# Seven half units of a normed activation turned by way of DRAM and VectorE in a fused two-layer decoder kernel

## The chip, the cores and the metric

The kernel runs on one core of a Trainium2 chip. TensorE (PE in the profile) multiplies matrices into PSUM; VectorE (DVE) and ScalarE (ACT) work on SBUF and PSUM; SyncE (SP) issues nearly all DMAs between DRAM and SBUF. Each engine takes its instructions in a fixed order and they wait for each other through semaphores. The metric is the device time of one execution in microseconds, the median of several runs.

## The reference

Two layers on 512 tokens of width 2048 in fp32: a layer of differential attention, then one projection of the stream into shared keys, values and forget gates, then a layer of forgetting attention.

```python
def shared_kv(x, c_act, w_mod_kv, b_mod_kv, w_kv, b_f):
    mod = c_act @ w_mod_kv + b_mod_kv
    shift, scale = jnp.split(mod, 2, axis=-1)
    hk = x * (1.0 + scale[:, None]) + shift[:, None]
    kvf = hk @ w_kv
    k, v, zf = jnp.split(kvf, [B_WIDTH, 2 * B_WIDTH], axis=-1)
    ...
    log_f = jax.nn.log_sigmoid(zf.astype(jnp.float32) + b_f.astype(jnp.float32))
    F = jnp.cumsum(log_f, axis=1)

for l in range(DEPTH):                                   # DEPTH = 2, N_A = 1
    h = x * (1.0 + scale[:, None]) + shift[:, None]
    if l < N_A:
        y = diff_attention(h, ...)
    else:
        if kv is None:
            kv = shared_kv(x, c_act, kv_w_mod, kv_b_mod, kv_w, kv_b_f)
        y = forgetting_attention(h, ..., *kv)
    x = layer_norm(DN_ALPHA * x + gate[:, None] * y, ln_g[l], ln_b[l])
```

The change lies at the seam: the layer norm that ends layer 0, and the first value columns of `hk @ w_kv`.

## The kernel before

**Products.** Every fp32 matrix product is made of three fp32r products: high part by high part, high by low, low by high (`products`, L227 to L231). A weight tile of 128x1024 comes from DRAM into `wst`, ScalarE casts its high part `whi` (L117), and VectorE makes the low part `wlo` = `wst` - `whi` (L118). `whi` and `wlo` have three buffers each, used in rotation.

**The normed activation.** The out projection of layer 0 ends with four token blocks of 128. For each, `norm_a(b)` (L1123) finds mean and 1/std, ScalarE norms the first 1024 columns of `n` (L1128) and VectorE the others (L1129), and SP stores the block to `n_dram` (L1130), from where layer 1's residual reads it much later.

**Turning.** The next product needs `n` with the 2048 features on the partitions. It is cut into 16 half units (half, s): half 0 or 1 is token blocks 0 and 1 or 2 and 3, and s is one of eight pairs of feature blocks. `build_half(s, half)` (L1132) turns a half unit's four 128x128 blocks on TensorE into one PSUM bank (L1140). For each of the two feature blocks ScalarE applies the modulation twice, once to fp32 (`htmp2`, L1148) and once to the high part `hh` (L1149), and VectorE makes the low part `hl` (L1150). At the end VectorE copies the turned blocks back into `n` (L1153), since layer 1 builds its own modulated activation from them later.

**Consuming.** The first group of value columns, `vj[0]`, takes the half units in the order of `lag` (L1156): (0,0), (0,1), (0,2), (0,3), (1,0), (1,1), (1,2), (0,4), (1,3), (0,5), (1,4), (0,6), (1,5), (0,7), (1,6), (1,7). I call the twelve matmuls of one half unit a step: two token blocks, two feature blocks, three products each. Before a step the loop (L1256) calls `build_next`, which builds a half unit that comes later in the order. Half 0 takes a weight tile, half 1 takes the same one a step or more later, and at the end of a half 1 step more weights are cast (`ws.advance`). Behind this group come the other value groups and, among their matmuls, the forget logits (L1221, L1222: 64 matmuls of the bank `zfp`).

**What sets the order.** Outside the kernel's first stage, which has an order written out by hand, the code's order is not yet the engines': a scheduler of the framework places each instruction in its engine's queue. So an edit at one place can also move instructions that it doesn't name.

Of the kernel before, what the change touches and what calls it, by code (L numbers as in the profile page):

```python
# [10 lines left out]
F32 = mybir.dt.float32  # L11
F32R = mybir.dt.float32r
I32 = mybir.dt.int32
AF = mybir.ActivationFunctionType
ALU = mybir.AluOpType

P = 128
D = 2048
# [147 lines left out]
def tile_yoco(  # L166
# [23 lines left out]
    nc = tc.nc  # L190
    V, S, PE, G = nc.vector, nc.scalar, nc.tensor, nc.gpsimd
# [13 lines left out]
    n_dram = dram.tile([T, D], F32, name="n_dram")  # L205
# [8 lines left out]
    def sc_bank(name="sc"):  # L214
        return ps.tile([P, 512], F32, name=name, tag="sc", bufs=2)
# [11 lines left out]
    def products(dst, lhs, rhs, start, stop):  # L227

        PE.matmul(dst, lhs[0], rhs[0], start=start, stop=False)  # L229
        PE.matmul(dst, lhs[0], rhs[1], start=False, stop=False)  # L230
        PE.matmul(dst, lhs[1], rhs[0], start=False, stop=stop)  # L231
# [120 lines left out]
    Hh = [None] * KT  # L352
    Hl = [None] * KT

    def new_h(kt):
        Hh[kt] = hpool.tile([P, T], F32R, name="hh", tag="H")
        Hl[kt] = hpool.tile([P, T], F32R, name="hl", tag="H")
# [149 lines left out]
    with tc.tile_pool(name="start", bufs=2, reuse_waits="tile") as sp, tc.manual_schedule(engines=engines):  # L507
# [6 lines left out]
        xts, loaded, accs, pms, turned, temps, banks, hi_of = {}, {}, {}, {}, {}, {}, {}, {}  # L514
# [528 lines left out]
    def moments(pool, stats, b):  # L1043
        mv = pool.tile([P, 2], F32, name="mv", tag="mv", bufs=4)
        V.bn_aggr(mv, stats[:, b, :, :])
        ve = pool.tile([P, 1], F32, name="lve", tag="lve", bufs=4)
        rstd = pool.tile([P, 1], F32, name="lrstd", tag="lrstd", bufs=4)
        V.tensor_scalar(ve, mv[:, 1:2], EPS, None, op0=ALU.add)
        rsqrt(rstd, ve, 1, pool)
        return mv, rstd  # L1050
# [41 lines left out]
    zp = []  # L1092

    ab = {}
# [28 lines left out]
    def norm_a(b):  # L1123
        pool, n, stats = zp
        mv, rstd = moments(pool, stats, b)
        mr = pool.tile([P, 1], F32, name="mr", tag="mr", bufs=4)
        V.scalar_tensor_tensor(mr, mv[:, 0:1], -1.0, rstd, op0=ALU.mult, op1=ALU.mult)
        S.activation(n[:, b, 0:1024], n[:, b, 0:1024], AF.Identity, scale=rstd, bias=mr)  # L1128
        V.tensor_scalar(n[:, b, 1024:], n[:, b, 1024:], mv[:, 0:1], rstd, op0=ALU.subtract, op1=ALU.mult)  # L1129
        nc.sync.dma_start(n_dram[b * P : (b + 1) * P, :], n[:, b, :])  # L1130

    def build_half(s, half):  # L1132

        pool, n, _ = zp
        px = sc_bank()
        hs = slice(256 * half, 256 * half + 256)
        for q in range(2):
            for b in range(2):
                src = n[:, 2 * half + b, (2 * s + q) * P : (2 * s + q + 1) * P]
                PE.transpose(px[:, q * 256 + b * P : q * 256 + (b + 1) * P], src, ident)  # L1140
        for q in range(2):
            kt = 2 * s + q
            if half == 0:
                new_h(kt)
            tmp = pool.tile([P, 256], F32, name="htmp2", tag="htmp2", bufs=2)
            pq = px[:, q * 256 : (q + 1) * 256]
            sc, sh = ab["kv"][0][:, kt : kt + 1], ab["kv"][1][:, kt : kt + 1]
            S.activation(tmp, pq, AF.Identity, scale=sc, bias=sh)  # L1148
            S.activation(Hh[kt][:, hs], pq, AF.Identity, scale=sc, bias=sh)  # L1149
            V.tensor_tensor(Hl[kt][:, hs], tmp, Hh[kt][:, hs].bitcast(F32), op=ALU.subtract)  # L1150

        place = n[:, 2 * half : 2 * half + 2, 2 * s * P : (2 * s + 2) * P].rearrange("p b (q t) -> p q b t", t=P)
        V.tensor_copy(place, px.rearrange("p (q b t) -> p q b t", q=2, b=2))  # L1153


    lag = [(0, 0), (0, 1), (0, 2), (0, 3), (1, 0), (1, 1), (1, 2)]  # L1156
# [5 lines left out]
    def build_next(n=1):  # L1162
        for _ in range(n):
            unit = next(built, None)
            if unit:
                build_half(unit[1], unit[0])

    pieces.extend(attention_a(A_HEADS - 1, 1))
    pieces.append(lambda: split_og((14, 15)))
    pieces.append(lambda: ab.update(kv=fold(0, ktile("mrow"))))  # L1170
    out_projection(oA, 0, zp, open_n, residual_a, norm_a, lambda b, k: build_next() if b == 3 and k < 2 else None)
    npool, n, nstats = zp

# [17 lines left out]
    def evac_v(g):  # L1191
        def fn(b, acc):
            vt = ktile("vt")
            S.copy(vt, acc)
            nc.scalar.dma_start(v_dram[b * P : (b + 1) * P, 512 * g : 512 * (g + 1)], vt)
        return fn
# [59 lines left out]
    for i, (half, s) in enumerate(lag):  # L1256
        if i != 2:
            build_next()
        if (half, s) == (0, 3):
            ws.step(lambda: kpool.tile([P, 512], F32R, name="held", tag="K"))  # L1260
            ws.load(ws.done + ws.STAGES - 1)
        if half == 0:
            held[s] = ws.get(vj[0], s, 0)
        hi, lo = held[s]
        for b in (2 * half, 2 * half + 1):
            bs = slice(b * P, (b + 1) * P)
            for kq in range(2):
                kt = 2 * s + kq
                products(acc[b], (Hh[kt][:, bs], Hl[kt][:, bs]), (hi[kq], lo[kq]), kt == 0, kt == KT - 1)
            if s == KT // 2 - 1:  # L1270
                evac_v(0)(b, acc[b])
        if half == 1:
            ws.advance(ws.where[id(vj[0]), s] + 4)
# [310 lines left out]
```

## Time and profile before

| | us |
|---|---|
| median of three runs | 1948.99 |
| lowest and highest run | 1948.52, 1949.28 |
| the profiled execution | 1947.43 |
| its span, first instruction to last | 1945.6 |
| TensorE busy in it | 1913.7 |
| VectorE busy | 1345.5 |
| ScalarE busy | 703.3 |

The span is what the trace shows; about 1.8 us of the profiled execution's time lie around it. Busy TensorE time is counted from modelled ends of pipelined matmuls, so it tells whether TensorE stood still, and the distance between two starts tells how long a matmul took. The stage in question lies near 990 to 1045 us of the span.

### The profile page before, as it was taken

How to read it: one execution, taken by the hardware profiler on the slowest of the kernel's cores; microseconds unless marked ns; L12 is line 12 of the kernel's file. 1: busy time of each engine (PE TensorE's matmuls, PEld its weight loads, DVE VectorE, ACT ScalarE, POOL GpSimd, SP SyncE). 2: the span in 40 equal slices, each digit the busy share in tenths (PEclk: the TensorE clock that was granted, in tenths of full speed). 3: DMA queues.
4: the chain of work that ended last, by engine and by line, in shares of the span. 5: the costliest groups of instructions: out<-in, count | busy, mean ns of one | idle time of the engine just before them, and what ended most of it. 6: DMA issues, size and time to landing. Idle time of an engine off the chain costs nothing.

```text
span 1945.6 us, 25043 instructions
## 1 busy us (share of the span) xinstructions
PE 1913.7 (98%) x8781; PEld 1588.8 (82%) x8781; DVE 1345.5 (69%) x2370; ACT 703.3 (36%) x1193; POOL 2.2 (0%) x10
## 2 busy tenths in 40 slices
PE   5999999999999999999999999999999999999997
PEld 4888888888888888888888888888888888888886
DVE  7995678877787778643575656566566666696657
ACT  3333434323333325531273222224334343453123
POOL 0000000000000000000000000000000000000000
PEclk9999999999999999999999999999999999999999
DMA  9993576877878784352346666664344555457522
GB/s 340 382 321 93 163 219 211 256 250 234 260 233 262 229 266 137 120 174 97 126 141 223 238 238 205 223 217 130 111 152 145 157 153 158 145 160 230 194 92 103
DMA packets 311162, 378.73 MB, mean 195 GB/s; under 512 B 58710, under 2 KB 228972, under 8 KB 310268
## 3 DMA queue, kind: packets, MB, share of 16 engines
q1 hardware_dynamic: 308608, 372.90, 59.7%
q10 hardware_dynamic: 2428, 4.23, 0.6%
q8 instruction: 69, 1.13, 0.2%
q14 instruction: 57, 0.47, 0.1%
HBM read 346.94 MB, written 30.10 MB: 194 GB/s over the span
## 4 chain that ended last, share of the span: by engine, by line
PE 95%; DVE 2%; DMA 1%; SPq 0%; issue 0%; ACT 0%; DVEq 0%; ACTq 0%
PE acc L229 27%; PE acc L230 27%; PE acc L231 27%; PE acc L677 4%; PE sc L679 2%; PE o L229 1%; PE sc L231 1%; PE sc L230 1%; PE o L231 1%; PE sc L229 1%; PE o L230 1%; PE o L679 1%; DMA sms<-in_w_mod_dram 1%; DVE wlo L118 0%; SPq L528 0%; PE tr L622 0%
## 5 line engine op out<-in xcount | busy, mean ns | idle before, releaser
L118 DVE TENSOR_TENSOR wlo<-wst,whi 128x1024 fp32r<-128x1024 f32 (+1 forms) x290 | 349.7, 1206 | 341.9 <-ACT whi L117 335.1
L117 ACT CAST whi<-wst 128x1024 fp32r<-128x1024 f32 (+1 forms) x290 | 301.6, 1040 | 669.1 <-PE acc L231 340.4
L229 PE MATMUL acc<-hh,whi 128*128 128x512 f32 x1184 | 463.4, 391 | 0.0
L230 PE MATMUL acc<-hl,whi 128*128 128x512 f32 x1184 | 461.6, 390 | 0.0
L231 PE MATMUL acc<-hh,wlo 128*128 128x512 f32 x1184 | 461.2, 389 | 0.0
L229 PE MATMUL acc<-whi,hh 128*128 128x512 f32 x1104 | 432.4, 392 | 0.0
L230 PE MATMUL acc<-wlo,hh 128*128 128x512 f32 x1104 | 430.5, 390 | 0.1
L231 PE MATMUL acc<-whi,hl 128*128 128x512 f32 x1104 | 430.1, 390 | 0.0
L231 PEld LDWEIGHTS acc<-hh,wlo 128*128 128x128 f32 x1184 | 222.3, 188 | 47.3
L229 PEld LDWEIGHTS acc<-hh,whi 128*128 128x128 f32 x1184 | 222.5, 188 | 43.0
L230 PEld LDWEIGHTS acc<-hl,whi 128*128 128x128 f32 x1184 | 222.6, 188 | 42.1
L231 PEld LDWEIGHTS acc<-whi,hl 128*128 128x128 f32 x1104 | 207.3, 188 | 43.4
L230 PEld LDWEIGHTS acc<-wlo,hh 128*128 128x128 f32 x1104 | 207.5, 188 | 41.7 <-DVE wlo L118 0.5
L229 PEld LDWEIGHTS acc<-whi,hh 128*128 128x128 f32 x1104 | 207.4, 188 | 41.5
L457 DVE SCALAR_TENSOR_TENSOR macc<-ms,cact,macc 128x1024 f32<-128x1024 f32 (+1 forms) x180 | 197.7, 1098 | 23.7 <-DMA ms<-in_kv_w_mod_dram 13.6
L568 DVE SCALAR_TENSOR_TENSOR sacc<-sms,cact,sacc 128x512 f32<-128x512 f32 x112 | 77.1, 745 | 3.5 <-DMA sms<-in_w_mod_dram 3.0
L804 ACT ACTIVATE e<-e,mn 128x128 f32<-128x128 f32 (+3 forms) x64 | 36.0, 563 | 102.5 <-DVE mn L800 102.4
L1386 ACT ACTIVATE eb<-eb,mnb 128x128 f32<-128x128 f32 (+1 forms) x64 | 36.1, 564 | 86.2 <-DVE mnb L1383 86.1
L677 PE MATMUL acc<-whi,hh 128*128 128x512 f32 x128 | 51.7, 407 | 0.0
L677 PE MATMUL acc<-wlo,hh 128*128 128x512 f32 x128 | 50.0, 391 | 1.6 <-DVE wlo L135 1.6
L126 ACT CAST whi<-wst 128x768 fp32r<-128x768 f32 (+1 forms) x30 | 28.3, 944 | 61.0 <-PE o L679 28.6
L677 PE MATMUL acc<-whi,hl 128*128 128x512 f32 x128 | 49.9, 390 | 0.0
(276 smaller groups left out, 1999.2 us busy)
## 6 DMA issues: line engine op xcount, KB each, us to landing
wst<-in_a_w_in_dram SPq DMA_DIRECT2D x237, 256.0 KB, 4.3
ms<-in_w_mod_dram SPq DMA_DIRECT2D x64, 512.0 KB, 4.6
ms<-in_kv_w_mod_dram SPq DMA_DIRECT2D x64, 512.0 KB, 4.5
wst<-in_kv_w_dram SPq DMA_DIRECT2D x64, 512.0 KB, 3.7
sms<-in_w_mod_dram SPq DMA_DIRECT2D x56, 512.0 KB, 7.5
wst<-in_b_w_in_dram SPq DMA_DIRECT2D x112, 256.0 KB, 2.9
wst<-in_a_w_out_dram SPq DMA_DIRECT2D x32, 512.0 KB, 3.7
msk<-in_w_mod_dram SPq DMA_DIRECT2D x64, 256.0 KB, 5.5
```

The lines of the kernel that those rows point to most:

```text
L117: self.nc.scalar.copy(hi[:, :, :w], st[:, :, :w])
L118: self.nc.vector.tensor_tensor(lo[:, :, :w], st[:, :, :w], hi[:, :, :w].bitcast(F32), op=ALU.subtract)
L126: self.nc.scalar.copy(hi[:, :, : job.width], self.stage[self.done][:, :, : job.width])
L229: PE.matmul(dst, lhs[0], rhs[0], start=start, stop=False)
L230: PE.matmul(dst, lhs[0], rhs[1], start=False, stop=False)
L231: PE.matmul(dst, lhs[1], rhs[0], start=False, stop=stop)
L457: ins = V.scalar_tensor_tensor(acc, w, cact[:, kt : kt + 1], acc, op0=ALU.mult, op1=ALU.add)
L568: V.scalar_tensor_tensor(acc, w, sc, acc, op0=ALU.mult, op1=ALU.add)
L677: PE.matmul(bank(v, b), h[:, bs], w, start=start, stop=stop)
L679: PE.matmul(bank(v, b), w[:, bs], h, start=start, stop=stop)
L804: S.activation(e[:, :w], e[:, :w], AF.Exp, bias=mn, scale=-1.0, accum_out=rs)
L1386: S.activation(e[:, :w], e[:, :w], AF.Exp, bias=mn, scale=-1.0, accum_out=rs)
```

## The change

For the seven half units (1,3), (1,4), (0,6), (1,5), (0,7), (1,6) and (1,7), TensorE no longer turns the blocks. A new function `fetch` loads the half unit back from `n_dram`, eight DMAs of 32x8x32 elements, each 256 runs of 128 bytes, 32 KB: this puts the 32x32 blocks of a 128x128 block in their turned places, and `build_far` has VectorE turn each 32x32 block within itself (L1152 of the new file) straight into `n`. ScalarE's two passes (L1160, L1161) then read `n` in SBUF instead of PSUM, VectorE makes `hl` (L1162), and the copy back falls away. The loop calls `fetch` four steps ahead; `nblk` has four buffers. The other nine half units are built as before, and 36 turns on TensorE are left of 64. Lastly, the last token block's norm on ScalarE is cut into two pieces of 512 columns, and its store into four.

```diff
@@ norm_a
-        S.activation(n[:, b, 0:1024], n[:, b, 0:1024], AF.Identity, scale=rstd, bias=mr)
+        cuts = (0, 1024) if b < 3 else (0, 512, 1024)
+        for f0, f1 in zip(cuts, cuts[1:]):
+            S.activation(n[:, b, f0:f1], n[:, b, f0:f1], AF.Identity, scale=rstd, bias=mr)
         V.tensor_scalar(n[:, b, 1024:], n[:, b, 1024:], mv[:, 0:1], rstd, op0=ALU.subtract, op1=ALU.mult)
-        nc.sync.dma_start(n_dram[b * P : (b + 1) * P, :], n[:, b, :])
+        cuts = (0, D) if b < 3 else (0, 512, 1024, 1536, D)
+        for f0, f1 in zip(cuts, cuts[1:]):
+            nc.sync.dma_start(n_dram[b * P : (b + 1) * P, f0:f1], n[:, b, f0:f1])
+
+    blocks = {}
+
+    def fetch(half, s):
+        t = blocks[half, s] = zp[0].tile([P, 512], F32, name="nblk", tag="nblk", bufs=4)
+        for q in range(2):
+            cs = 256 * s + 128 * q
+            src = n_dram[256 * half : 256 * half + 256, cs : cs + 128].rearrange("(m c) (a r) -> a c m r", c=32, a=4)
+            for a in range(4):
+                to = t[32 * a : 32 * a + 32, 256 * q : 256 * q + 256].rearrange("c (m r) -> c m r", m=8)
+                nc.sync.dma_start(to, src[a])
+
+    def build_far(s, half):
+        pool, n, _ = zp
...
+        turned = n[:, 2 * half : 2 * half + 2, 2 * s * P : (2 * s + 2) * P].rearrange("p b (q t) -> p q b t", t=P)
+        V.transpose(turned, t.rearrange("p (q b t) -> p q b t", q=2, b=2))
+        for q in range(2):
...
+            place = n[:, 2 * half : 2 * half + 2, kt * P : (kt + 1) * P]
...
+            S.activation(tmp.rearrange("p (b t) -> p b t", b=2), place, AF.Identity, scale=sc, bias=sh)
+            S.activation(Hh[kt][:, hs].rearrange("p (b t) -> p b t", b=2), place, AF.Identity, scale=sc, bias=sh)
+            V.tensor_tensor(Hl[kt][:, hs], tmp, Hh[kt][:, hs].bitcast(F32), op=ALU.subtract)
 
     def build_half(s, half):
-
+        if (half, s) in blocks:
+            return build_far(s, half)
...
@@ the loop over lag
         if i != 2:
             build_next()
+        for unit in lag[i + 4 : i + 5]:
+            if unit[1] >= (6, 3)[unit[0]]:
+                fetch(*unit)
```

The engines' orders change in this stage alone. ScalarE's queue around half unit (0,7), before: `sc_9114` is the PSUM bank of (0,7), `hh_9119` and `hh_9125` its high parts, `whi_9144` the next weights, `sc_9150` the bank of (1,6).

```order
L1148 ACTIVATE htmp2_9121<-sc_9114,mod_b0_7745,mod_a0_7744 128x256
L1149 ACTIVATE hh_9119<-sc_9114,mod_b0_7745,mod_a0_7744 128x256
L1148 ACTIVATE htmp2_9127<-sc_9114,mod_b0_7745,mod_a0_7744 128x256
L1149 ACTIVATE hh_9125<-sc_9114,mod_b0_7745,mod_a0_7744 128x256
L117 CAST whi_9144<-wst_8962 128x1024
L1148 ACTIVATE htmp2_9155<-sc_9150,mod_b0_7745,mod_a0_7744 128x256
L1149 ACTIVATE hh_9057<-sc_9150,mod_b0_7745,mod_a0_7744 128x256
```

The cast stands behind all four instructions of (0,7). ScalarE's queue at the same place after: `hh_9021` and `hh_9027` are the high parts of (1,5), `hh_9162` is the first of (0,7), and `whi_9186` takes the buffer whose last reader is the step (1,5).

```order
L1160 ACTIVATE htmp2_9132<-n_7765,mod_b0_7745,mod_a0_7744 128x256
L1161 ACTIVATE hh_9021<-n_7765,mod_b0_7745,mod_a0_7744 128x256
L1160 ACTIVATE htmp2_9136<-n_7765,mod_b0_7745,mod_a0_7744 128x256
L1161 ACTIVATE hh_9027<-n_7765,mod_b0_7745,mod_a0_7744 128x256
L117 CAST whi_9186<-wst_8984 128x1024
L1160 ACTIVATE htmp2_9164<-n_7765,mod_b0_7745,mod_a0_7744 128x256
L1161 ACTIVATE hh_9162<-n_7765,mod_b0_7745,mod_a0_7744 128x256
```

The cast now stands ahead of (0,7). It is the same two steps earlier (cast `whi_9125`, after step (1,4), ahead of (0,6)) and two steps later (cast `whi_9240`, after step (1,6), ahead of (1,7)); on VectorE `wlo_9187`, made from `whi_9186`, stands ahead of the turn of (0,7).

TensorE's queue at the end of step (1,5), before: `acc_8761` is the bank of the last token block, `acc_8758` of the first, and `sc_9150` takes the turns of (1,6).

```order
L229 MATMUL acc_8761<-whi_8958,hh_9001 128x512
L230 MATMUL acc_8761<-wlo_8959,hh_9001 128x512
L231 MATMUL acc_8761<-whi_8958,hl_9002 128x512
L1140 MATMUL sc_9150<-ident_79,n_7765 128x128 x4
L229 MATMUL acc_8758<-whi_9082,hh_9119 128x512
L230 MATMUL acc_8758<-wlo_9083,hh_9119 128x512
```

The turns of (1,6) stand between steps (1,5) and (0,7). TensorE's queue there after: `acc_8765` is the last token block's bank, `zfp_9285` that of the forget logits, and `hh_9162` comes from ScalarE's queue above.

```order
L229 MATMUL acc_8765<-whi_8980,hh_9027 128x512
L230 MATMUL acc_8765<-wlo_8981,hh_9027 128x512
L231 MATMUL acc_8765<-whi_8980,hl_9028 128x512
L1254 MATMUL zfp_9285<-hh_9021,zp64_8756 128x512
L1255 MATMUL zfp_9285<-hl_9022,zp64_8756 128x512
L1254 MATMUL zfp_9285<-hh_9027,zp64_8756 128x512
L1255 MATMUL zfp_9285<-hl_9028,zp64_8756 128x512
L229 MATMUL acc_8762<-whi_9125,hh_9162 128x512
L230 MATMUL acc_8762<-wlo_9126,hh_9162 128x512
```

The turns are gone, and four matmuls of forget logits have come forward from the next group. Others have moved likewise: 20 stand after step (1,4) and four after step (1,6), where the queue goes on with one matmul each into two banks of the next group on `whi_9240` and then one on `wlo_9241`. Between steps (0,7) and (1,6) stand twelve matmuls of the next group on `whi_9186` and `wlo_9187`.

SP's queue, before, from the store of the last token block (`n_dram_72<-n_7765`) on; `wst` are weight loads.

```order
L56 DMA wst_8926<-in_kv_w_dram 128x2x512
L1130 DMA n_dram_72<-n_7765 128x2048
L56 DMA wst_8962<-in_kv_w_dram 128x2x512
L56 DMA wst_9024<-in_kv_w_dram 128x2x512
L56 DMA wst_9086<-in_kv_w_dram 128x2x512
L56 DMA wst_9148<-in_kv_w_dram 128x2x512
```

Weight loads follow the store at once. SP's queue from the same place after: `nblk` is a half unit that `fetch` brings.

```order
L56 DMA wst_8939<-in_kv_w_dram 128x2x512
L1134 DMA n_dram_72<-n_7765 128x512 x4
L1145 DMA nblk_8888<-n_dram_72 32x8x32 x8
L1145 DMA nblk_8959<-n_dram_72 32x8x32 x8
L56 DMA wst_8984<-in_kv_w_dram 128x2x512
L1145 DMA nblk_8995<-n_dram_72 32x8x32 x8
L1145 DMA nblk_9034<-n_dram_72 32x8x32 x8
L56 DMA wst_9059<-in_kv_w_dram 128x2x512
L1145 DMA nblk_9070<-n_dram_72 32x8x32 x8
L1145 DMA nblk_9104<-n_dram_72 32x8x32 x8
L56 DMA wst_9129<-in_kv_w_dram 128x2x512
L1145 DMA nblk_9140<-n_dram_72 32x8x32 x8
```

The store is four DMAs, and the 56 fetches stand among the weight loads, `wst_8984` (the source of `whi_9186`) behind the second unit of eight.

## Rows read from the trace of the kernel before

**Rows 1.** The page: busy time of each engine, its share, its instructions.

```profile
PE 1913.7 (98%) x8781; PEld 1588.8 (82%) x8781; DVE 1345.5 (69%) x2370; ACT 703.3 (36%) x1193; POOL 2.2 (0%) x10
```

**Rows 2.** Windows: us, busy PE, PEld, DVE, ACT, POOL, clock, DMA share, GB/s.

```profile
1000.00:1030.00 30.00, 30.00 (x151) 24.72 (x150) 18.34 (x33) 23.18 (x43) 0.00 (x0) 1.00 0.34 105
1060.00:1925.00 865.00, 864.91 (x3912) 718.12 (x3912) 559.17 (x961) 293.79 (x467) 0.00 (x0) 1.00 0.54 171
```

**Rows 3.** Timeline of TensorE: start, us, engine, line, operation, tiles [idle before].

```profile
987.06 0.39 PE L229 MATMUL acc<-whi,hh 128*128 128x512 f32 x1
...
989.78 0.27 PE L1140 MATMUL sc<-ident,n 128*128 128x128 f32 x1
...
1003.08 0.60 PE L1140 MATMUL sc<-ident,n 128*128 128x128 f32 x4
1003.44 0.48 PE L229 MATMUL acc<-whi,hh 128*128 128x512 f32 x1
...
1006.30 0.60 PE L1140 MATMUL sc<-ident,n 128*128 128x128 f32 x4
```

**Rows 4.** Groups of VectorE by shape: count, busy us, mean ns, idle before.

```profile
L486 DVE STREAM_TRANSPOSE mturn<-macc 128x512 f32<-128x512 f32 x24 | 17.0, 706 | 0.3
...
L911 DVE STREAM_TRANSPOSE e<-og 128x512 f32<-128x512 f32 x14 | 15.3, 1095 | 0.0
```

**Rows 5.** Timelines of TensorE and ScalarE at the last block's norm.

```profile
990.59 0.39 PE L229 MATMUL acc<-held,hh 128*128 128x512 f32 x1
991.13 0.55 PE L1140 MATMUL sc<-ident,n 128*128 128x128 f32 x3 [0.15 <-ACT n L1128]
...
989.83 1.25 ACT L1128 ACTIVATE n<-n,mr,lrstd 128x1024 f32<-128x1024 f32 x1 [3.29 <-DVE mr L1127]
```

**Rows 6.** Timelines of TensorE and ScalarE at a weight cast and a half unit.

```profile
1015.95 0.60 PE L1140 MATMUL sc<-ident,n 128*128 128x128 f32 x4
1016.14 1.05 ACT L117 CAST whi<-wst 128x1024 fp32r<-128x1024 f32 x1 [0.84 <-PE acc L231]
...
1010.15 0.57 ACT L1148 ACTIVATE htmp<-sc,mod_b,mod_a 128x256 f32<-128x256 f32 x1 [1.27 <-PE sc L1140]
1010.61 0.56 ACT L1149 ACTIVATE hh<-sc,mod_b,mod_a 128x256 fp32r<-128x256 f32 x1
```

**Rows 7.** Timeline of VectorE behind that cast.

```profile
1017.23 1.23 DVE L118 TENSOR_TENSOR wlo<-wst,whi 128x1024 fp32r<-128x1024 f32 x1 [0.87 <-ACT whi L117]
...
1018.37 0.42 DVE L1150 TENSOR_TENSOR hl<-htmp,hh 128x256 fp32r<-128x256 f32 x1
```

**Rows 8.** Timeline of SP's queue: start, us of all, issues (x).

```profile
991.10 0.34 SPq L1130 DMA_DIRECT2D n_dram<-n  x1
...
1409.21 1.81 SPq L1407 DMA_DIRECT2D pTl<-turned  x4
```

**Rows 9.** DMA issues, 1390 to 1700 us: KB each, median us to landing.

```profile
turned<-tb SPq DMA_DIRECT2D x12, 256.0 KB, 2.1
...
pTl<-turned SPq DMA_DIRECT2D x48, 16.0 KB, 2.2
```

**Rows 10.** Windows near the start and the end, columns as in rows 2.

```profile
21.20:23.00 1.80, 1.79 (x4) 1.38 (x5) 1.14 (x2) 1.80 (x4) 0.00 (x0) 1.00 0.96 330
36.28:37.85 1.57, 0.00 (x0) 0.00 (x0) 1.57 (x3) 0.18 (x1) 0.00 (x0) 1.00 1.09 382
1933.53:1936.70 3.17, 0.00 (x0) 0.00 (x0) 3.00 (x6) 0.46 (x2) 0.00 (x0) 1.00 0.63 256
1936.80:1936.85 0.05, 0.00 (x0) 0.00 (x0) 0.05 (x1) 0.05 (x1) 0.00 (x0) 0.50 0.00 0
```

**Rows 11.** Timeline of TensorE: start, and its last matmul.

```profile
25.51 0.39 PE L679 MATMUL sc<-hh,wlo 128*128 128x512 f32 x1
...
1933.14 0.39 PE L231 MATMUL acc<-held,hl 128*128 128x512 f32 x1
```

**Rows 12.** Line L528: issue time on SP, ns min/median/max, first and last start.

```profile
L528 SPq DMA_DIRECT2D sms<-in_w_mod_dram x72: 367/1035/2250, 1.2 to 128.2; - x72
```

More of the change, by code (lines that the diff above doesn't have):

```diff
@@ L1127, in norm_a @@
         V.scalar_tensor_tensor(mr, mv[:, 0:1], -1.0, rstd, op0=ALU.mult, op1=ALU.mult)
-        S.activation(n[:, b, 0:1024], n[:, b, 0:1024], AF.Identity, scale=rstd, bias=mr)
+        cuts = (0, 1024) if b < 3 else (0, 512, 1024)
+        for f0, f1 in zip(cuts, cuts[1:]):
+            S.activation(n[:, b, f0:f1], n[:, b, f0:f1], AF.Identity, scale=rstd, bias=mr)
         V.tensor_scalar(n[:, b, 1024:], n[:, b, 1024:], mv[:, 0:1], rstd, op0=ALU.subtract, op1=ALU.mult)
-        nc.sync.dma_start(n_dram[b * P : (b + 1) * P, :], n[:, b, :])
+        cuts = (0, D) if b < 3 else (0, 512, 1024, 1536, D)
[12 more added lines that the diff above has]
+        pool, n, _ = zp
+        hs = slice(256 * half, 256 * half + 256)
+        t = blocks.pop((half, s))
+        turned = n[:, 2 * half : 2 * half + 2, 2 * s * P : (2 * s + 2) * P].rearrange("p b (q t) -> p q b t", t=P)
+        V.transpose(turned, t.rearrange("p (q b t) -> p q b t", q=2, b=2))
+        for q in range(2):
+            kt = 2 * s + q
+            if half == 0:
+                new_h(kt)
+            place = n[:, 2 * half : 2 * half + 2, kt * P : (kt + 1) * P]
+            tmp = pool.tile([P, 256], F32, name="htmp2", tag="htmp2", bufs=2)
+            sc, sh = ab["kv"][0][:, kt : kt + 1], ab["kv"][1][:, kt : kt + 1]
+            S.activation(tmp.rearrange("p (b t) -> p b t", b=2), place, AF.Identity, scale=sc, bias=sh)
+            S.activation(Hh[kt][:, hs].rearrange("p (b t) -> p b t", b=2), place, AF.Identity, scale=sc, bias=sh)
+            V.tensor_tensor(Hl[kt][:, hs], tmp, Hh[kt][:, hs].bitcast(F32), op=ALU.subtract)
     def build_half(s, half):
+        if (half, s) in blocks:
+            return build_far(s, half)
         pool, n, _ = zp
```

## Prediction

> **What bounds the kernel now.** I read the page's busy times first [rows 1]: TensorE is busy 1913.7 of 1945.6 us. Then two windows [rows 2]: through the stage that is changed, from 1000 to 1030 us, TensorE is busy 30.00 of 30 us at a granted clock of 1.00, and from 1060 to 1925 us 864.91 of 865. So a microsecond of TensorE's time saved or lost in the stage comes out at the end. No other engine sets the pace there (VectorE 18.34, ScalarE 23.18 of 30), but they can make TensorE wait. The timeline of TensorE [rows 3] shows what the turning costs: four turns of 128x128 stand ahead of a step's 12 matmuls, and the pattern repeats after 3.22 us (1003.08, 1006.30). Without turns between them 12 matmuls took 2.72 us (987.06 to 989.78), which is 0.227 each.
>
> **What the change takes away.** Seven half units lose four turns each. A set costs at least 0.36 us, from its start to the next matmul's (1003.08 to 1003.44), and at most 3.22 - 2.72 = 0.50 us [rows 3]. I take 0.47, near the upper end because the period holds everything, also the slower matmul behind the turns (0.48 where others take 0.39): 7 x 0.47 = **3.3 us**, between 2.5 and 3.5.
>
> VectorE's rate is no term. It loses seven copies out of PSUM and gains seven 32x32 turns of 128x512, at 0.706 us (L486, which like the new one writes runs of 32) or, at worst, 1.095 (L911) [rows 4]: 7 us of work on an engine that is idle for 12 of these 30 us. Its order matters, below.
>
> The Trainium skill, page "VectorE: DVE Perf Modes", section "Rules for kernel authors", speaks against this change: it gives the 128x128 turn to TensorE wherever PSUM will do as the target, since VectorE turns only inside 32x32 blocks. Its price of 390 ns for a turn in bf16 would make 28 of them worth an estimated 10.9 us. The trace disagrees: 0.36 us are four, not one.
>
> **The last block in pieces.** TensorE starts a matmul at 990.59 and the next three turns at 991.13, behind ScalarE's norm of 1024 columns, 1.25 us from 989.83 [rows 5]. One interval of 0.23 after 990.59 is 990.82, so 0.31 us are lost. Now the turns need only the first 512 columns: half of 1.25 after 989.83 is 990.5. But a unit's turns stand two matmuls earlier in the new order, so TensorE arrives at 990.36 and waits some 0.2. Gain **0.1 us** (0 to 0.3).
>
> **What it adds: two holes from the order.** This is the step that decides. A step needs ScalarE's `hh` of its half unit; ScalarE and VectorE work in order. Before, the cast of the next weights stood behind the half unit that TensorE needs first; after, it stands ahead of it (ScalarE's two fences in the change). The cast writes one of three `whi` buffers, whose last reader is the step just before. So nothing of the next half unit can start until that step is done, ScalarE has cast, VectorE has made `wlo`, and VectorE has turned the block, since the turn stands behind `wlo` in its queue. Counted from the time T at which TensorE could go on:
> the cast starts 0.19 after T (1016.14 against 1015.95) and lasts 1.05 [rows 6]; `wlo` starts 0.04 later (1017.23) and VectorE's next instruction 1.14 after that (1018.37) [rows 7]; the turn 0.71; some 0.05 to ScalarE; `htmp` to `hh` 0.46 (1010.15 to 1010.61); `hh` 0.56 [rows 6]; 0.05 to TensorE (norm's end at 991.08, turns at 991.13 [rows 5]). Sum 4.25 us, of which I take **4.2**, between 3.7 (ScalarE's two, 1.02 us, at two thirds, since they now read SBUF, and the handoffs gone) and 4.6 (the turn at 1.095).
>
> TensorE can fill with forget logits, matmuls of the same size at 0.227 us, which stood in the next group and cost nothing by being moved.
> - After (1, 4) stand 20 of them, 4.5 us: the chain of 4.2 is covered. Cost 0, at most 0.1.
> - After (1, 5) stand 4, 0.9 us, and then the step (0, 7). Hole A: 4.2 - 0.9 = **3.3 us** (2.8 to 3.7).
> - After (1, 6) stand 4, then matmuls of the next group on the newly cast weights. `whi` is ready at 0.19 + 1.05 + 0.05 = 1.3, so 0.4 is lost; two matmuls run, to 1.75; `wlo` is ready at 0.19 + 1.05 + 0.04 + 1.23 + 0.05 = 2.55, so 0.8 more is lost. Hole B: **1.2 us** (1.0 to 1.4). Unit (1, 7) is built behind it, in time.
>
> In the trace of before the only idle of TensorE that a row of the stage names is the 0.15 us of [rows 5].
>
> **The fetch itself.** 56 DMAs join SP's queue, each 256 runs of 128 bytes, 32 KB. The nearest rows: four DMAs of 16 KB with such runs issue in 1.81 us, 0.45 each [rows 8], and 16 KB ones land after 2.2 us, as the 256 KB ones do after 2.1 [rows 9]. I take 0.47 each, 3.8 us for a unit's eight. The first waits for the stores of the last block, issued from 991.10 on [rows 8] and landed some 3 us later: about 994. Unit (1, 3) is whole at 994 + 3.8 + 2.2 = 1000; its step begins near 1006 and its turn is wanted near 1004. Unit (1, 7) is whole at 994 + 7 x 3.8 + 3 x 0.4 for weight loads + 2.2 = 1024; VectorE comes to it near 1040, 3 us after (1, 6) ends at 1037 (from 1006: five steps of 2.72, one set of turns and 4.5 of logits to the end of (1, 5), 0.9 of logits, hole A, and three times 2.72 for (0, 7), twelve matmuls of the next group and (1, 6)). Cost 0. Behind the fetches wait weight loads: `wst_8984`, between the second and third unit, is issued near 1002 and cast after (1, 5), near 1025. Cost 0.
>
> **The sum.** -3.3 - 0.1 + 3.3 + 1.2 = **+1.1 us**, own range -0.0 (-3.8 + 3.8) to +2.7 (-2.5 + 5.2). The profiled execution took 1947.43 us (span 1945.6), 1.56 us under the median of the runs, 1948.99; a change in TensorE's stream adds to both alike. Forecast 1948.99 + 1.1 = **1950.1 us**, from 1949.0 to 1951.7. A measurement of this kernel can tell about 0.2%, 3.9 us, from no change; so I forecast no difference that shows.
>
> **Rivals.**
> *The holes stay shut.* If ScalarE or VectorE come earlier than I think, or TensorE finds work, only the gain is left: 1948.99 - 3.4 = 1945.6 us. For it: TensorE lost almost nothing here before. Against: the cast cannot start before (1, 5) is done, and each instruction behind it has a row. Chance 0.09; a gain beyond 3.9 us would need turns that cost more than their period [rows 3]: 0.03.
> *The clock falls in hole A* (slower, in its upper part). TensorE stood still for 1.57 us at 36.28 and kept 1.00 (2.4 GHz). After its last matmul, started at 1933.14 [rows 11], it had 1.00 until at least 1936.70 and 0.50 (1.2 GHz) by 1936.80 [rows 10], 3.4 us after the next matmul could have started. Hole A is to be 3.3, with 3.7 as its upper end, so it decides from 0.1 us more than I think. Its price: at the kernel's start matmuls are slow until about 25.5 (four in 21.20 to 23.00, 0.45 us each [rows 10]; the first of the usual 0.39 at 25.51 [rows 11]), 4.3 us in which half the time is lost, or twice that if the earlier ones count: 1950.1 + 2.2 to 4.3 = 1952.3 to 1954.4. Against: the hole must come out long, and 1.57 left no mark. Chance 0.18, two thirds of it above 1952.9.
> *The fetch is late* (slower). It decides from the price c of one DMA on SP: the last unit is late when 994 + 56 c + 4 exceeds 1040, from c = 0.75 us. [rows 12] has a median of 1.035 for the start's mod loads, with the DMA engines near full; at that price the unit lands at 1056, 16 us late, and the time is near 1966. Against: the DMA engines are 34% busy in the stage [rows 2], and the nearest form costs 0.45. Chance 0.08.
> The Trainium skill, "DMA: Bandwidth & Descriptors", section "Measured", says that transfers under 64 KB are bound by their descriptors and gives 0.95 us for 64 KB; 56 of those one behind the other would make this rival true, at an estimated 1961 us. The rows agree as far as 16 KB take as long to land as 256 KB, but four issue in 1.81 us.
>
> **How the numbers follow.** The forecast has 0.58, all of it "same"; the remaining 0.04 is what I don't see in the next group, where loads change places, spread evenly. Same: 0.58 + 0.09 + 0.06 of the clock's case + 0.02 = 0.75. Slower: 0.12 + 0.08 + 0.01 = 0.21. Faster: 0.03 + 0.01 = 0.04. The range 1946.0 to 1954.0 takes in the forecast, half of the shut holes and most of the clock's case, about 0.8.
>
> **What would show it.** TensorE's waits should name ScalarE's `hh` (new line L1161) once for about 3 us, near 1026, and ScalarE's cast and VectorE's `wlo` for about 1 us near 1038; none near 1019 to 1024. Turns of TensorE in the stage: 36, no longer 64. The last of the 56 fetches should be issued before 1025. VectorE's turn (L1152) should take 0.71 us and wait for `wlo`, not for a DMA. If it waits for DMAs, the third rival holds; if the granted clock after hole A is below 1, the second; if TensorE is busy throughout, the first. I am wrong in the chain if hole A is under 2.5 or over 4 us.

## The result, and the profile after

The changed kernel took 1954.01 us, median of 11 runs (1951.12 to 1957.03), beside 1948.99 for the kernel before: a ratio of 1.0026, 95% interval 1.0018 to 1.0035, or 3.5 to 6.8 us slower. Forecast were 1950.1 us, 1946.0 to 1954.0, and no difference that shows. The profiled execution took 1952.09 us, its span 1950.3. The page's busy line, which answers to [rows 1]:

```profile
PE 1915.4 (98%) x8753; PEld 1587.9 (81%) x8753; DVE 1346.1 (69%) x2370; ACT 704.1 (36%) x1194; POOL 2.2 (0%) x10
```

The 28 turns are gone (8781 matmuls are now 8753), yet TensorE is busy 1.7 us longer. That difference lies ahead of the changed stage (972.0 us busy up to the stage's start, where the kernel before had 970.3). In the stage itself TensorE is busy 89.2 us, before 89.4: matmuls at half clock, and the slower ones at each stop, count as busy and make up for the turns. So the total says nothing of the change. To see what the stage itself gained or lost I take two points that both orders have: its first matmul on the held weights, and ScalarE's first copy of the second value group, before and behind which TensorE's order is the same in both. Between them stand the same 362 matmuls of 512 columns. Before, then after, TensorE's and ScalarE's timelines:

```profile
989.81 0.47 PE L229 MATMUL acc<-held,hh 128*128 128x512 f32 x1
...
1079.35 0.59 ACT L1194 COPY vt<-acc 128x512 f32<-128x512 f32 x1 [0.30 <-PE acc L231]
```

```profile
990.34 0.47 PE L229 MATMUL acc<-held,hh 128*128 128x512 f32 x1
...
1083.84 0.59 ACT L1227 COPY vt<-acc 128x512 f32<-128x512 f32 x1 [0.30 <-PE acc L231]
```

The stage took 89.54 us before and 93.50 after: 3.96 us more. (It also began 0.53 us later, which lies in the kernel's first stages and is not the change's: over all profiles of all kernels here it began anywhere from 989.7 to 993.5 us.) The named waits of TensorE in the stage, where before there was one of 0.15 us [rows 5]:

```profile
PE acc L229 <- ACT hh L1161: 3.3, 1, 3.3
PE acc L230 <- DVE wlo L118: 0.5, 1, 0.5
PE acc L229 <- ACT whi L117: 0.2, 1, 0.2
```

They are the two holes of the prediction: the first is hole A, the other two are hole B. The timeline of TensorE shows what lies around them:

```profile
1022.34 0.39 PE L231 MATMUL acc<-whi,hl 128*128 128x512 f32 x1
1022.81 0.50 PE L229 MATMUL acc<-whi,hh 128*128 128x512 f32 x1
...
1023.38 0.40 PE L231 MATMUL acc<-whi,hl 128*128 128x512 f32 x1
1023.80 0.50 PE L229 MATMUL acc<-whi,hh 128*128 128x512 f32 x1
...
1026.68 0.39 PE L1255 MATMUL zfp<-hl,zp 128*128 128x512 f32 x1
1030.34 0.79 PE L229 MATMUL acc<-whi,hh 128*128 128x512 f32 x1 [3.27 <-ACT hh L1161]
1030.93 0.63 PE L230 MATMUL acc<-wlo,hh 128*128 128x512 f32 x1
1031.36 0.63 PE L231 MATMUL acc<-whi,hl 128*128 128x512 f32 x1
...
1041.55 0.73 PE L229 MATMUL acc<-whi,hh 128*128 128x512 f32 x2 [0.21 <-ACT whi L117]
1042.81 0.50 PE L230 MATMUL acc<-wlo,hh 128*128 128x512 f32 x1 [0.53 <-DVE wlo L118]
```

The chain behind hole A, in the timelines of ScalarE and then VectorE:

```profile
1026.17 1.05 ACT L117 CAST whi<-wst 128x1024 fp32r<-128x1024 f32 x1 [2.43 <-PE acc L231]
1029.20 0.60 ACT L1160 ACTIVATE htmp<-n,mod_b,mod_a 128x256 f32<-128x256 f32 x1 [1.98 <-DVE n L1152]
1029.70 0.58 ACT L1161 ACTIVATE hh<-n,mod_b,mod_a 128x256 fp32r<-128x256 f32 x1
...
1027.25 1.23 DVE L118 TENSOR_TENSOR wlo<-wst,whi 128x1024 fp32r<-128x1024 f32 x1 [3.05 <-ACT whi L117]
1028.40 0.70 DVE L1152 STREAM_TRANSPOSE n<-nblk 128x512 f32<-128x512 f32 x1
```

Cast, `wlo`, turn, `htmp`, `hh`: each starts when the one before it is done or nearly so, in the order that the prediction wrote out, and TensorE resumes at 1030.34, 0.06 us after `hh`.

And the windows around hole A (columns as in rows 2):

```profile
1026.91:1030.28 3.37, 0.16 (x1) 0.00 (x0) 1.85 (x2) 1.40 (x4) 0.00 (x0) 1.00 0.00 0
1030.30:1033.70 3.40, 3.36 (x8) 2.69 (x9) 1.51 (x3) 0.97 (x2) 0.00 (x0) 0.50 0.00 0
1033.72:1040.00 6.28, 6.28 (x28) 5.07 (x28) 0.85 (x2) 3.25 (x6) 0.00 (x0) 1.00 0.37 113
```

TensorE's granted clock falls to 0.50 (1.2 GHz) just as it resumes after hole A, stays there for 3.4 us, and the matmuls start 0.43 us apart (1030.93 to 1031.36) in place of 0.23.

Taken with the usual 0.23 us from start to start, the stage's losses are: hole A 3.43 (1026.68 to 1030.34, less 0.23); the low clock 1.68 (eight matmuls to 1033.84, with the slower first one that follows any stop); hole B 1.29 (the two stops and their slower first matmuls); and 0.84 in stops too short for a named wait, 0.66 before (1,5) (1022.34 to 1022.81, 1023.38 to 1023.80) and 0.18 before (1,4). That is 7.24 us. The stage is 3.96 longer, so a gain of 3.28 us is left for the seven sets of turns, 0.47 each. This gain is a remainder and not measured by itself; two kernels below give it independently.

### The profile page after: what moved, and what is told of

Its sections match the earlier page's. It is cut to its first block, busy times and chain, and to the rows that moved or that the text cites. A ratio compares the mean times of both kernels' runs of the same rounds, so it can differ in the third digit from the quotient of the medians.

```text
span 1950.3 us, 25079 instructions
## 1 busy us (share of the span) xinstructions
PE 1915.4 (98%) x8753; PEld 1587.9 (81%) x8753; DVE 1346.1 (69%) x2370; ACT 704.1 (36%) x1194; POOL 2.2 (0%) x10
## 4 chain that ended last, share of the span: by engine, by line
PE 95%; DVE 2%; DMA 2%; SPq 1%; ACT 0%; issue 0%; DVEq 0%; ACTq 0%
PE acc L229 27%; PE acc L230 27%; PE acc L231 27%; PE acc L677 4%; PE sc L679 2%; PE o L229 1%; PE sc L231 1%; PE o L231 1%; PE sc L230 1%; PE sc L229 1%; PE o L230 1%; PE o L679 1%; DMA sms<-in_w_mod_dram 1%; DVE wlo L118 0%; SPq L528 0%
```

## The experiments

The table gives for each kernel the stage as above, how long TensorE stood still before (0,7) (from start to start, less 0.23; the idle time that a timeline prints in brackets is 0.16 less), how long the granted clock was at 0.50 behind it, the median time, and the ratio to the kernel before on the same chip. The kernels ran on several chips, so medians are best compared by this ratio.

| kernel | stage, us | standstill | low clock | median, us | ratio (95%) |
|---|---|---|---|---|---|
| before | 89.54 | 0 | 0 | 1948.99 | |
| changed | 93.50 | 3.43 | 3.41 | 1954.01 | 1.0026 (1.0018 to 1.0035) |
| again | 93.41 | 3.43 | 3.41 | 1954.42 | 1.0028 (1.0018 to 1.0038) |
| again2, one run | 94.44 | 3.44 | 6.83 | 1955.80 | |
| again3, one run | 93.49 | 3.43 | 3.41 | 1951.19 | |
| again4, one run | 93.48 | 3.43 | 3.41 | 1953.28 | |
| lower_behind | 89.89 | 1.37 | 0 | 1949.64 | 1.0003 (0.9994 to 1.0012) |
| gap30 | 92.16 | 2.98 | 3.41 | 1952.49 | 1.0013 (1.0004 to 1.0022) |
| gap29 | 93.77 | 3.62 | 6.83 | 1952.89 | 1.0019 (1.0010 to 1.0028) |
| longer | 94.04 | 3.45 and 0.9 | 3.41 | 1953.42 | 1.0025 (1.0016 to 1.0034) |
| gap44 | 94.09 | 5.05 | 3.41 | 1955.31 | 1.0032 (1.0020 to 1.0044) |
| behind | 87.42 | 0 | 0 | 1947.22 | 0.9993 (0.9984 to 1.0002) |
| seven7 | 86.58 | 0 | 0 | 1946.09 | 0.9989 (0.9980 to 0.9998) |
| pieces | 89.42 | 0 | 0 | 1948.79 | 0.9996 (0.9987 to 1.0005) |

### The order alone: lower_behind

One instruction is moved, VectorE's `wlo` behind the turn and the `hl` of (0,7):

```diff
-            self.nc.vector.tensor_tensor(lo[:, :, :w], st[:, :, :w], hi[:, :, :w].bitcast(F32), op=ALU.subtract)
+            lower = self.nc.vector.tensor_tensor(lo[:, :, :w], st[:, :, :w], hi[:, :, :w].bitcast(F32), op=ALU.subtract)
+            if self.pin:
+                self.pin(lower)
...
+            ws.pin = tc.keep_in_program_order if s == 5 else None
             ws.advance(ws.where[id(vj[0]), s] + 4)
+            ws.pin = None
```

> The changed kernel with one instruction moved: VectorE's wlo made from the cast behind step (1,5) now stands behind the turn and the two hl of (0,7), no longer ahead of them; the casts stay where they are. Chain theory: the turn runs beside the cast, so hole A shrinks from 3.4 to about 1.5 us (cast to 1.25 after the step's end, htmp and hh another 1.1, less 0.9 of logits). Clock theory: with 1.5 us of standstill the clock stays at 1.00 and its cost goes too: 1954.0 - 2.0 - 1.6 or more, 1949.4 to 1950.0, with runs no further apart than those of the kernel before (some 3 us). Rival (the clock has nothing to do with hole A): only the 2.0 us go, 1952, and the runs stay 6 us apart.

Timelines of TensorE, ScalarE and VectorE, and then windows, of lower_behind:

```profile
1028.73 0.39 PE L1258 MATMUL zfp<-hl,zp 128*128 128x512 f32 x1
1030.33 0.50 PE L232 MATMUL acc<-whi,hh 128*128 128x512 f32 x1 [1.20 <-ACT hh L1164]
...
1028.23 1.05 ACT L118 CAST whi<-wst 128x1024 fp32r<-128x1024 f32 x1 [2.44 <-PE acc L234]
1029.18 0.60 ACT L1163 ACTIVATE htmp<-n,mod_b,mod_a 128x256 f32<-128x256 f32 x1
...
1031.64 1.22 DVE L119 TENSOR_TENSOR wlo<-wst,whi 128x1024 fp32r<-128x1024 f32 x1
```

```profile
1028.96:1030.33 1.37, 0.17 (x2) 0.01 (x1) 0.02 (x1) 1.37 (x4) 0.00 (x0) 1.00 0.00 0
1030.33:1039.00 8.67, 8.67 (x38) 6.94 (x39) 3.44 (x6) 4.28 (x9) 0.00 (x0) 1.00 0.34 93
```

`htmp` now starts right behind the cast, since the turn is long done; `wlo` comes last, at 1031.64. The standstill shrank by 2.06 us and the stage by 3.61: the other 1.55 is the low clock, which is gone. TensorE's order in the stage is the same in both kernels. So one instruction's place in VectorE's queue was worth 3.6 us in the profiles, and 4.8 between the medians on the same chip (1954.42 in again, 1949.64). That the wait for `wlo` and the turn were links of the chain is shown by this; the cast's link is shown by behind, below.

### Holes closed: behind, and seven7

In behind both the casts and the `wlo` from step (1,4) on are held behind the half unit that TensorE needs next:

```diff
-            self.nc.scalar.copy(hi[:, :, :w], st[:, :, :w])
+            cast = self.nc.scalar.copy(hi[:, :, :w], st[:, :, :w])
+            if self.pin:
+                self.pin(cast)
...
+            ws.pin = tc.keep_in_program_order if s >= 4 else None
```

> The changed kernel with its casts and wlo from step (1,4) on held behind the half unit that TensorE needs next, on ScalarE and on VectorE, as in the kernel before; fetch and VectorE's turns stay. My theory (the holes come from the order alone): waits on hh, on the cast and on wlo vanish to below 0.5 us in all, the clock stays at 1.00, and what is left is the gain of seven sets of turns, 3.2 us, less small waits: 1945.5 to 1946.8, faster than the kernel before by 0.1 to 0.2%. Rival (the fetch is late and the order only hid it): TensorE then waits for turns that wait for DMAs, most likely before (1,7), whose last fetches were issued at 1037 us, and the time is 1948 or more.

The stage took 87.42 us, 2.12 less than before, and the clock stayed at 1.00. The median is 1947.22, somewhat over the 1945.5 to 1946.8 expected, and the interval of its ratio includes 1. What is missing is a part of the rival: TensorE lost 1.1 us before (1,7), its hl and hh late behind a turn that waited 1.28 us for a DMA. Timelines of TensorE, VectorE, ScalarE's DMA queue and SP's:

```profile
1037.29 0.50 PE L234 MATMUL acc<-whi,hh 128*128 128x512 f32 x1 [0.51 <-ACT hh L1166]
...
1035.33 0.71 DVE L1157 STREAM_TRANSPOSE n<-nblk 128x512 f32<-128x512 f32 x1 [1.28 <-DMA nblk<-n_dram]
...
1031.11 0.36 ACTq L1233 DMA_DIRECT2D v_dram<-vt  x1
...
1022.97 10.74 SPq L1150 DMA_DIRECT2D nblk<-n_dram  x8
```

The last unit's eight fetches were issued over 10.74 us, where other units take 4. The instructions' waits show why: SP's DMAs and ScalarE's take turns on eight completion semaphores, and one of the last fetches waits for the semaphore of a store of v, which ScalarE issues only after step (0,7). In behind two of the last fetches wait so, the longer for 7.0 us. In the changed kernel that store was issued at 1034.65 us and the fetch that waits for its semaphore at 1036.93 (SP's timeline):

```profile
1013.21 7.95 SPq L1145 DMA_DIRECT2D nblk<-n_dram  x16
...
1021.75 15.97 SPq L1145 DMA_DIRECT2D nblk<-n_dram  x8
```

There the turn of (1,7) stood behind `wlo` until 1042.67 us anyway, so this delay cost nothing. seven7 issues the last unit right behind the one before it:

```diff
-        for unit in lag[i + 4 : i + 5]:
+        for unit in (lag[14:16] if i == 10 else () if i == 11 else lag[i + 4 : i + 5]):
```

> behind (casts behind the half unit that is needed next) with one edit more: the last unit's fetch, (1,7), is issued right after (1,6)'s, ahead of a weight load. In behind it was the one late unit: its last DMAs were issued at 1033 us, after ScalarE's store of v, and TensorE lost 1.1 us before (1,7). My theory: that wait goes too, and what is left is the gain of the turns, 3.2 us, less 0.3 us of small waits: 1.0 to 1.2 us under behind, 1945.4 to 1946.2. Rival (the last unit is late because 56 fetches take SP's time, not for where it stands): a wait of 0.5 us or more before (1,7) or (1,6) stays and the time is within 0.5 us of behind.

The stage took 86.58 us, 2.96 less than before and 0.84 less than behind, and no wait of TensorE in it is named but the one for the norm. SP's timeline of seven7:

```profile
1013.25 18.66 SPq L1150 DMA_DIRECT2D nblk<-n_dram  x24
```

The semaphore is still shared: the last two fetches again waited for a store of v, 6.1 us, which is why 24 issues took 18.66 us, and VectorE's turn of (1,7) waited 0.69 us for its data. The edit did not end this wait, as I had expected it to; it only brought the data early enough that TensorE lost 0.2 us before (1,7) in place of 1.1. The rival, that the 56 fetches need SP's time, is not borne out: SP spent the time waiting. The gain of the turns is nearly all there: 2.96 us net here, and 2.12 + 1.1 = 3.2 in behind, beside the 3.28 that was left as a remainder. The median is 1946.09, ratio 0.9989 with an interval of 0.9980 to 0.9998: faster than the kernel before by a margin that this measurement just resolves.

### The clock: again, longer, gap29, gap44, gap30

`again` to `again4` are the changed kernel unaltered. In `longer` ScalarE writes the first `htmp` of (0,7) three times, in gap44 the first `hh` three times; gap29 and gap30 are lower_behind with four and three `hh`. The edit of gap44, the others likewise:

```diff
-            S.activation(Hh[kt][:, hs].rearrange("p (b t) -> p b t", b=2), place, AF.Identity, scale=sc, bias=sh)
+            for _ in range(3 if (half, s, q) == (0, 7, 0) else 1):
+                S.activation(Hh[kt][:, hs].rearrange("p (b t) -> p b t", b=2), place, AF.Identity, scale=sc, bias=sh)
```

> The changed kernel once more, nothing altered, to see a second profiled execution of it. In the first one the clock fell to half for 3.4 us behind hole A and cost 1.6 us; the holes cost 4.8 and small ones 0.8, the turns gave 3.2. My theory (the clock falls in hole A, and for how long differs from execution to execution): the same waits to within 0.1 us (ScalarE's hh 3.3, ScalarE's cast 0.2, VectorE's wlo 0.5), times spread over some 5 us, 1951 to 1957, and a low clock behind hole A of another length than 3.4 us may show. Rival (the waits themselves vary): hole A or B differs by 1 us or more from the first profile, and the low clock is again 3.4 us.

Its waits were the same to 0.1 us and its low clock too. Two profiles do not tell why the changed kernel's runs lie 6 us apart.

> The changed kernel with hole A made longer: ScalarE writes the first htmp of (0,7) three times over, two extra instructions of 0.5 us between the cast and hh. Hole A 4.4 us, 1.0 more. If the clock stays low for a set time from its fall, part of it now lies in the standstill and the kernel loses about 0.5 us more than the changed kernel, 1954.5. If it stays low for a set amount of work, it loses the whole 1.0 us, 1955.0. If the length of the standstill beyond 3.4 us makes the low clock longer, it loses 2 us or more, 1956 and up.

The edit missed: the scheduler put the extra `htmp` behind the first `hh`, so hole A stayed and a second stop of 0.9 us came right after it. But it showed something. TensorE's timeline of `longer`:

```profile
1031.63 0.50 PE L229 MATMUL acc<-whi,hh 128*128 128x512 f32 x1 [3.28 <-ACT hh L1162]
1031.97 0.39 PE L230 MATMUL acc<-wlo,hh 128*128 128x512 f32 x1
...
1033.57 0.79 PE L231 MATMUL acc<-whi,hl 128*128 128x512 f32 x1 [0.74 <-DVE hl L1163]
```

After a standstill of 3.45 us the matmuls still ran at full clock, and it fell only at 1033.58, behind the second stop.

> lower_behind (hole A 1.36 us, no fall of the clock) with ScalarE writing the first hh of (0,7) four times over, three extra instructions of 0.49 us between the turn and TensorE: hole A 2.8 to 2.9 us. If the clock falls only when the standstill reaches about 3.4 us, it stays at 1.00 and the cost is the 1.5 us alone: 1951.1. If shorter standstills do it too, it falls and another 1.6 us or so are lost: 1952.7.

> The changed kernel with the first hh of (0,7) written three times over, two extra instructions of 0.49 us ahead of TensorE's next matmul, so that hole A itself is longer (in the run before, the extra htmp went behind it): 4.4 us. If the clock falls 3.4 us after the stop and is low for 3.4 us, 1.0 us of that lies in the standstill, so slow matmuls cost 1.1 to 1.2 us instead of 1.6: 0.5 us more than the changed kernel, 1954.7. If it is low for as much work as before, 1.0 us more, 1955.2.

Both standstills came out longer than meant, 3.62 and 5.05 us, since each rewrite of `hh` waits for the one before it (0.62 us from start to start) and the scheduler put the second `htmp` ahead of them. So gap29 did not test a standstill below 3.4; it gave a low clock of 6.83 us instead, for a standstill only 0.2 us longer than hole A. gap44's low clock was 3.41 us, of which 0.24 lay in the standstill; neither of its two prices is separated by the medians. In gap29, gap44 and gap30 the edit also moved matmuls of TensorE behind (0,7), and hole B is not there. So their stages and medians differ from the others' by more than the standstill; what they show is in their profiles, the stop and the clock.

> The changed kernel, unaltered, for another profiled execution. Waits as before (hh 3.3, cast 0.2, wlo 0.5 us). Two profiles of it had the clock low for 3.4 us behind hole A, at a cost of 1.6 us; gap29, with a standstill only 0.2 us longer, had it low for 6.8. Theory (the same standstill meets the clock differently in each execution): among three more profiles at least one shows a low clock of about 6.8 us, costing 3 us or more, or none at all, and the time moves with it. Rival (always 3.4 us; the spread of the times is elsewhere): all three show 3.4 us and differ in time by what lies before 990 us.

> The same once more, with the same two expectations: a low clock of another length than 3.4 us in at least one of the three, or 3.4 us in all.

> The same for the third time, with the same two expectations.

The windows of again2, and then of again4:

```profile
1029.96:1032.12 2.16, 0.16 (x1) 0.00 (x0) 1.81 (x2) 0.32 (x1) 0.00 (x0) 1.00 0.00 0
1032.20:1033.40 1.20, 0.00 (x1) 0.01 (x1) 0.02 (x1) 1.15 (x3) 0.00 (x0) 0.50 0.00 0
1033.40:1038.90 5.50, 5.50 (x13) 4.34 (x14) 1.49 (x3) 1.52 (x3) 0.00 (x0) 0.50 0.04 14
```

```profile
1027.85:1031.28 3.43, 0.16 (x2) 0.00 (x1) 1.87 (x3) 1.46 (x4) 0.00 (x0) 1.00 0.01 2
1031.28:1032.20 0.92, 0.92 (x4) 0.71 (x5) 0.40 (x1) 0.92 (x2) 0.00 (x0) 1.00 0.00 0
1032.30:1035.60 3.30, 3.30 (x9) 2.53 (x8) 1.03 (x2) 0.59 (x1) 0.00 (x0) 0.50 0.00 0
```

The theory held for the clock: the same stop meets it differently. In again2 the clock fell 2.2 us after the stop and was low for 6.83 us; in again4 it fell 4.4 us after the stop, when TensorE had been running for 0.9 us. The standstill was the same 3.43 us to 0.01 in all five profiles of this program, and the clock fell in all five, after 2.2, 3.3, 3.4, 3.8 and 4.4 us. For the spread of the times the rival is nearer: again2's stage is 0.9 to 1.0 us longer than the others', not 3, but it began at 993.39 us and that of again3, the fastest of the five, at 989.72. Of the 4.6 us between these two, 3.7 lie ahead of the stage.

> gap29 with one hh fewer: ScalarE writes the first hh of (0,7) three times over. In gap29 three extra hh made hole A 3.6 us (not 2.9), since the second htmp came between; one fewer should give 3.0 to 3.1 us. In seven profiles a standstill of 3.4 to 5.1 us always brought the clock down, 2.2 to 5.4 us after the stop, and 1.4 us never did. If 3.0 us are still below what brings it down: clock 1.00 in the profile, and the runs lie 1.7 us above lower_behind's 1949.64, near 1951.3, no further apart than the kernel before's. If 3.0 us bring it down too, always or sometimes: a low clock of 3.4 or 6.8 us in the profile or runs at 1953 and above, median 1952.5 or more.

Windows of gap30:

```profile
1029.20:1032.17 2.97, 0.16 (x1) 0.00 (x0) 0.02 (x1) 2.94 (x7) 0.00 (x0) 1.00 0.66 188
1032.17:1033.40 1.23, 1.23 (x5) 0.97 (x6) 1.17 (x3) 0.44 (x1) 0.00 (x0) 1.00 0.07 27
1033.50:1036.90 3.40, 3.40 (x10) 2.63 (x9) 1.75 (x3) 2.63 (x6) 0.00 (x0) 0.50 0.33 46
```

A standstill of 2.98 us brought the clock down too, 1.3 us after TensorE had resumed. Its median, 1952.49, was just under the 1952.5 that I had set for this answer; the profile decides it. The value 3.4 us on which the prediction rested is no limit.

Shorter stops are in these traces as well, in the kernel's first stage, where TensorE waits for a `wlo` near 37 us: the stop of 1.57 us in [rows 10]. Its length differs from profile to profile, and none of the edits here touches that stage. TensorE's timeline of pieces, and the windows before and behind:

```profile
38.13 0.50 PE L677 MATMUL acc<-wlo,hh 128*128 128x512 f32 x1 [1.75 <-DVE wlo L135]
```

```profile
38.10:38.70 0.60, 0.56 (x2) 0.48 (x3) 0.60 (x2) 0.60 (x1) 0.00 (x0) 1.00 1.09 384
38.80:42.10 3.30, 3.30 (x10) 2.52 (x9) 3.27 (x5) 0.00 (x0) 0.00 (x0) 0.50 1.09 383
```

In the five profiles in which TensorE was idle there for 1.75 to 2.43 us (pieces, gap30, again2, again4, gap44) the clock fell to 0.50 at 38.3 to 40.2 us and stayed there for 3.41; in the nine with 0.45 to 1.57 us it stayed at 1.00. By these traces hole A, idle for 3.27 us, was well beyond the shortest stop behind which the clock fell.

### The last block in pieces alone

```diff
-        S.activation(n[:, b, 0:1024], n[:, b, 0:1024], AF.Identity, scale=rstd, bias=mr)
+        cuts = (0, 1024) if b < 3 else (0, 512, 1024)
+        for f0, f1 in zip(cuts, cuts[1:]):
+            S.activation(n[:, b, f0:f1], n[:, b, f0:f1], AF.Identity, scale=rstd, bias=mr)
```

> The kernel before with the last block's norm in two pieces and its store in four, and nothing else of the change. In the profile of the changed kernel the first piece of 512 columns took 0.8 us, not half of 1.25, and TensorE lost 0.32 us there as before (0.31). So: no difference, 0 to -0.1 us; TensorE's wait for ScalarE's norm stays at 0.15 to 0.25 us. Rival (the pieces pay as forecast): 0.1 to 0.3 us less and a shorter wait.

The stage is 0.12 us shorter and the time the same. ScalarE's timeline of pieces shows both halves:

```profile
991.31 1.52 ACT L1130 ACTIVATE n<-n,mr,lrstd 128x512 f32<-128x512 f32 x2 [3.30 <-DVE mr L1127]
```

They take 1.52 us together where the whole took 1.25 [rows 5].

## Why the prediction was wrong, step by step

- **The turns.** Forecast 3.3 us, 0.47 a set; 3.28 as the remainder of the sum, 3.2 in behind, and 2.96 net in seven7. Right. VectorE's seven turns took 0.70 to 0.71 us, as taken from [rows 4]; ScalarE's passes from SBUF took 0.59, not less than the 0.56 from PSUM [rows 6]; that they might take two thirds, a bound of the chain, no run shows.
- **The pieces.** Forecast 0.1 us; TensorE lost 0.32 us at this place before and after, and 0.33 in pieces, so nothing was gained: half the columns took more than half the time.
- **Hole A.** Forecast 3.3 us (2.8 to 3.7), measured 3.43, by the chain that was written out and at the place that was named. Right; the timelines show the chain, and lower_behind and behind that it is the cause.
- **Hole B.** Forecast 1.2, measured 1.29. Right.
- **After (1,4).** Forecast 0 to 0.1, measured 0.84 before (1,4) and (1,5). A step that failed, though a small one: the 20 logits cover the chain to (0,6), but I did not follow the same late chain on to (1,5), whose turn stands behind the `hl` of (0,6) in VectorE's queue. Its `hh` ended at about 1022.8 us, when TensorE had been free since 1022.57. The next unit behind a late one is late too.
- **The clock.** This is the step that failed. I named it as a rival with its place and its price (2.2 to 4.3 us; measured 1.6 in four profiles, and 1 us more in the fifth), but gave it 0.18, because I took one row, a fall 3.4 us after the last matmul [rows 10], for the point from which it decides, and put hole A just under that. The runs show no such point: in all nine profiles with a standstill of 3.0 to 5.1 us before (0,7) the clock fell, 2.2 to 5.4 us after the stop began, and in the first stage it fell behind all five stops with 1.75 us of idle time or more. It did not fall behind 1.20 us idle (lower_behind), nor behind the 1.57 of [rows 10]. So the forecast hole, anywhere in its range of 2.8 to 3.7 us, was a case for the low clock, and its cost belonged into the sum. It was put at nothing there and measured 1.68.
- **The fetch.** Forecast as hidden, and in the changed kernel it was, at 0.49 us an issue (16 in 7.95) against 0.47, landing after 2.0. But the last fetch was issued near 1037 us, not before 1025 as I wrote: a queue that shares its semaphores with another engine's stores was not in the reckoning. In behind it cost 1.1 us.

Summed, -3.28 + 3.43 + 1.29 + 0.84 + 1.68 is +3.96 us, the stage's own difference; it closes because the first term is the remainder. Without the clock and the small stops the terms give 1.4, against +1.1 forecast. The medians differ by 5.0 us, more than the stage in four of the five profiles (3.9 to 4.0) and as much as in the fifth (4.9). Low clocks of both lengths among the runs would give a part of that, but how often each occurs was not counted, since a run without a profile lists only a mean clock (0.995 to 0.997 in the 11 runs). Where the last 1.1 us of the medians come from stays open.

That the change "moves work off TensorE" was true and worth its 3.3 us. What it cost came from the order: the scheduler placed casts and `wlo` ahead of the half unit, and these wait for the very step behind which TensorE then stands still. Why it placed them so, no run here shows.

## What to carry to other kernels

When work leaves the busiest engine for others, compare the order of what stands ahead of the moved work on those engines: an instruction there that waits for a buffer of the busy engine's last step turns into a stop of that engine, here 3.4 us for one cast and one subtraction. Holding those two behind the half unit, and fetching the last unit earlier, turned a loss of 5 us into a gain of 2 to 3 (seven7: 2.1 by the ratio, 2.96 in the stage). And a stop of TensorE is to be priced with the clock: in these traces every stop with 1.75 us of idle time or more was followed by matmuls at half clock, which cost another 1.6 us or more behind hole A. Look for such stops in all profiles of a kernel, since one profile can mislead: the kernel before showed a stop of 1.57 us that kept its clock, and pieces, alike up to there, one of 1.75 that lost it.

## What the runs showed of the hardware that I had not expected

- The granted clock's fall is not tied to the stop's length alone. The same program, stopped for the same 3.43 us, lost its clock 2.2 to 4.4 us after the stop began, sometimes while TensorE was already running again, and kept it low for 3.41 us in four profiles and for 6.83 in one. The Trainium skill, page "TensorE: Matmul & The Clock Gate", section "What's actually happening", says that the gate keeps a time of its own that does not start with the kernel, and that the transition point therefore shifts between runs. These five profiles agree with that: the fall moved by 2.2 us. Stops between 1.57 and 1.75 us of idle time, and whether each stop above that brings the clock down, are beyond these 14 profiles.
- ScalarE's passes over 128x256 that write the same tile again started 0.62 us apart (gap29), those with different targets 0.49.
- A DMA of 32 KB in 256 runs of 128 bytes took SP 0.49 us from one issue to the next and landed after 2.0 us (median), so that 56 of them fitted beside the weight loads; what delayed the last of them was a semaphore shared with ScalarE's stores (11.1 us of waiting in the changed kernel), not their number.
